# Attention values in two passes, with the row sums of the probabilities taken out of the value product

## The chip, the cores and the metric

The kernel runs on one core of a Trainium2 chip. The metric is the device time of one execution in microseconds (us), lower is better; the median of three runs is given. A core has a matrix engine (TensorE, PE in the profile; PEld is its weight load), a vector engine (VectorE, DVE), an activation engine (ScalarE, ACT), a general engine (GpSimd, POOL) and an engine that issues most transfers (SyncE, SP). Each engine works through its own queue in order; semaphores hold an instruction until those on other engines that it needs are done, and whatever stands behind it on its own queue is held too.

## The reference

A small encoder with two layers on a sequence of 1024 tokens, width 1024, in float32. Layer 0 mixes tokens with a chunked gMLP, layer 1 with chunked attention; each is followed by a gated convolutional feed-forward network. The change touches only the attention of layer 1, with 16 heads of 64 dimensions, where each chunk of 64 queries attends to its own chunk and the 8 chunks before it:

```python
sc = jnp.einsum('bqhd,bkhd->bhqk', qb, kb).astype(jnp.float32) + bias
valid = (start - PAD + jnp.arange(BAND)) >= 0
sc = jnp.where(valid[None, None, None, :], sc, NEG_INF)
p = jax.nn.softmax(sc, axis=-1).astype(vb.dtype)
return jnp.einsum('bhqk,bkhd->bqhd', p, vb)
```

For each query, softmax needs the sum of the exponentials over its keys, and the output is the value product divided by that sum.

## The kernel before

TensorE multiplies in a fast format with fewer mantissa bits (fp32r). To keep float32's accuracy, an operand is split into a high part (the value rounded to the format) and a low part (what is left), and a product is made of three passes: high x high, high x low, low x high. The helper `split` (L137) does this with a cast on ACT (L139) and a subtraction, mostly on DVE (L140).

The attention stage goes over the 16 heads in pairs, since two heads of 64 dimensions fill the 128 partitions: `c` is 0 for the even head of a pair and 1 for the odd one, and `rows[c]` gives the 64 partitions that are its own and the 64 that are the other's. Within a head the loop (from L1396 on) goes over 8 blocks of 128 keys. For a block, `Head.score` makes the scores of up to 640 queries on PE (tile `st`, L1256 and L1258), adds the position bias on DVE for the two near blocks (tile `p`, L1262), takes the exponential on ACT (L1263, L1266), and splits the result: `ph` by ACT (L1269), `pl` by POOL (L1270). Two blocks later (`LAG`) `Head.value` multiplies `ph` and `pl` with the values into the output accumulators `po`, one for each half `t` of the 1024 queries. In between, PE gets work that depends on nothing here: the matmuls `qkv` of the next pair's projections (L181, L184, L188), about 12 per block in an even head and 6 in an odd one, and the matmuls `mx` (L1210, L1217) for the next head's row maxima, which DVE reduces (tiles `junk`, `mb` at L1213, `ma` at L1219).

The order of PE's instructions is written out by hand, with a small clock (`tick`) and work that is put off by some microseconds (`put_off`); the order on DVE, ACT and POOL is set by a scheduler from what each instruction depends on. PSUM has eight tiles here: two for `po`, two for the projections and four (`psS`) that scores, maxima and transposes share. PE can write into one of the four only when its reader on DVE or ACT is done.

In the value product a block takes three passes: VH x ph, VL x ph, VH x pl. VH is 128 columns wide and holds the high part of V in the head's own 64 columns and 1.0 in the other 64; VL holds the low part and 0.0. So the other 64 rows of `po` collect the sums of the probabilities at no extra cost. The transposed V comes from PE four blocks at a time (`vtr`, L1182) and is written by `transpose_v` (L1187, L1188) straight into the even head's tiles; for the odd head it goes to narrow tiles first and from there by transfer (`stage_v`). When a half of a head is done, `Pair.done` copies one row of sums (ACT, L1311) and the head's 64 output rows (DVE, L1315) out of `po`, and after the odd head the sums are turned, inverted, broadcast and multiplied in, and the result is split and stored for the output projection. Three times in a pair POOL also multiplies new weights with their gains (tile `raw`, L159).

## Time and profile before

| | |
|---|---|
| median of 3 runs | 2132.54 us (2130.45 to 2134.04) |
| the profiled execution | 2131.62 us, its span 2129.5 us |
| granted TensorE clock | 0.999 of full speed |
| PE busy | 2116.1 us, 99% of the span |
| DVE busy | 1546.9 us, 73% |
| ACT busy | 1066.3 us, 50% |
| POOL busy | 744.6 us, 35% |
| attention stage | from about 975 to 1409 us |

The profile names a group by line, engine, operation, the tile written and the tiles read, with the shape; `x12` is a count. In the timeline each row starts with the start in us and the duration. Matmuls overlap in the pipeline, and their ends are modelled: how much time one takes is read from the distance of the starts. "Idle before" in brackets is how long the engine had waited, and for whom.

### The profile page before, as it was taken

How to read it: one execution, taken by the hardware profiler on the slowest of the kernel's cores; microseconds unless marked ns; L12 is line 12 of the kernel's file. 1: busy time of each engine (PE TensorE's matmuls, PEld its weight loads, DVE VectorE, ACT ScalarE, POOL GpSimd, SP SyncE). 2: the span in 40 equal slices, each digit the busy share in tenths (PEclk: the TensorE clock that was granted, in tenths of full speed). 3: DMA queues.
4: the chain of work that ended last, by engine and by line, in shares of the span. 5: the costliest groups of instructions: out<-in, count | busy, mean ns of one | idle time of the engine just before them, and what ended most of it. 6: DMA issues, size and time to landing. Idle time of an engine off the chain costs nothing.

```text
span 2129.5 us, 28843 instructions
## 1 busy us (share of the span) xinstructions
PE 2116.1 (99%) x9944; PEld 1771.8 (83%) x9944; DVE 1546.9 (73%) x2313; ACT 1066.3 (50%) x1878; POOL 744.6 (35%) x528
## 2 busy tenths in 40 slices
PE   9999999999999999999999999999999999999998
PEld 8888878888888888878888888888888888888887
DVE  4188789888888857676565665665988888885576
ACT  6333555554445544555555555643645544454443
POOL 1075644332334412054444543421323323342020
PEclk9999999999999999999999999999999999999999
DMA  7267733454445966635555455762244545578653
GB/s 252 80 203 253 242 104 99 139 188 140 172 162 194 299 254 219 238 110 139 132 135 127 127 127 135 186 214 108 79 148 135 187 134 174 164 278 303 213 188 129
DMA packets 181450, 367.86 MB, mean 173 GB/s; under 512 B 42908, under 2 KB 43292, under 8 KB 181304
## 3 DMA queue, kind: packets, MB, share of 16 engines
q1 hardware_dynamic: 177128, 358.47, 52.6%
q10 hardware_dynamic: 4176, 7.55, 1.0%
q8 instruction: 78, 1.28, 0.3%
q14 instruction: 68, 0.56, 0.1%
HBM read 233.12 MB, written 103.40 MB: 158 GB/s over the span
## 4 chain that ended last, share of the span: by engine, by line
PE 93%; DVE 4%; ACT 1%; issue 1%; DMA 0%; POOL 0%; SPq 0%; DVEq 0%; POOLq 0%; ACTq 0%
PE up L995 10%; PE gate L995 10%; PE up L375 7%; PE up L377 7%; PE up L380 7%; PE gate L375 5%; PE gate L380 5%; PE gate L377 5%; PE vps L510 4%; PE qkv L184 4%; PE qkv L181 4%; PE qkv L188 4%; PE ups L181 1%; PE po L1290 1%; PE st L1256 1%; PE po L1288 1%
## 5 line engine op out<-in xcount | busy, mean ns | idle before, releaser
L140 DVE TENSOR_TENSOR wlo<-raw,whi 128x512 fp32r<-128x512 f32 (+1 forms) x395 | 346.5, 883 | 179.7 <-ACT whi L139 179.3
L139 ACT CAST whi<-raw 128x512 fp32r<-128x512 f32 (+1 forms) x395 | 245.1, 623 | 281.1 <-PE gate L995 197.4
L375 PE MATMUL up<-yh,whi 128*128 128x512 f32 x688 | 268.1, 390 | 0.7 <-ACT gate L886 0.6
L377 PE MATMUL up<-yh,wlo 128*128 128x512 f32 x688 | 267.8, 389 | 0.0
L847 POOL TENSOR_TENSOR h<-a 128x512 f32<-128x512 f32 x44 | 82.0, 1864 | 403.3 <-DVE a L839 390.7
L1270 POOL TENSOR_TENSOR pl<-p,ph 128x640 fp32r<-128x640 f32 (+4 forms) x128 | 159.7, 1250 | 173.2 <-ACT ph L1269 128.0
L375 PE MATMUL gate<-th,whi 128*128 128x512 f32 x496 | 192.9, 389 | 0.0
L377 PE MATMUL gate<-th,wlo 128*128 128x512 f32 x496 | 192.9, 389 | 0.0
L380 PE MATMUL up<-yl,whi 128*128 128x512 f32 x688 | 184.2, 389 | 0.0
L375 PEld LDWEIGHTS up<-yh,whi 128*128 128x128 f32 x688 | 129.2, 188 | 28.9 <-ACT gate L886 2.0
L380 PEld LDWEIGHTS up<-yl,whi 128*128 128x128 f32 x688 | 129.1, 188 | 27.3 <-POOL yl L140 0.5
L377 PEld LDWEIGHTS up<-yh,wlo 128*128 128x128 f32 x688 | 129.2, 188 | 26.6
L140 DVE TENSOR_TENSOR yl<-raw,yh 128x512 fp32r<-128x512 f32 x172 | 143.1, 835 | 8.5 <-ACT yh L139 8.1
L184 PE MATMUL qkv<-yh,wlo 128*128 128x512 f32 x336 | 134.3, 400 | 0.0
L380 PE MATMUL gate<-tl,whi 128*128 128x512 f32 x496 | 132.8, 389 | 0.2 <-DVE tl L140 0.2
L181 PE MATMUL qkv<-yh,whi 128*128 128x512 f32 x336 | 132.4, 394 | 0.0
L139 ACT CAST whi<-S 128x512 fp32r<-128x512 f32 x160 | 99.2, 620 | 66.2 <-PE up L380 60.3
L140 DVE TENSOR_TENSOR wlo<-S,whi 128x512 fp32r<-128x512 f32 x160 | 130.6, 817 | 0.0
L995 PE MATMUL up<-yl,whi 128*128 128x512 f32 (+1 forms) x312 | 120.6, 387 | 0.0
L995 PE MATMUL gate<-yh,wlo 128*128 128x512 f32 (+1 forms) x312 | 120.4, 386 | 0.0
L995 PE MATMUL up<-yh,whi 128*128 128x512 f32 (+1 forms) x312 | 120.4, 386 | 0.0
L995 PE MATMUL up<-yh,wlo 128*128 128x512 f32 (+1 forms) x312 | 120.3, 386 | 0.0
(307 smaller groups left out, 5263.7 us busy)
## 6 DMA issues: line engine op xcount, KB each, us to landing
raw<-in_f_win SPq DMA_DIRECT2D x88, 512.0 KB
gT<-h SPq DMA_DIRECT2D x88, 256.0 KB
h<-in_f_wdown SPq DMA_DIRECT2D x44, 512.0 KB
dS<-h SPq DMA_DIRECT2D x88, 256.0 KB
raw<-dS SPq DMA_DIRECT2D x40, 512.0 KB
raw<-gT SPq DMA_DIRECT2D x40, 512.0 KB
gB<-a SPq DMA_DIRECT2D x66, 256.0 KB
raw<-in_f_wdown SPq DMA_DIRECT2D x30, 512.0 KB
```

Of the source, the lines that this page charges most:

```text
L139: behind[S] = S.copy(hi, src)
L140: return eng.tensor_tensor(lo, src, f32(hi), op=ALU.subtract)
L181: nc.tensor.matmul(ps, wh[:, k, :], xs[k][0], start=k == 0, stop=False)
L184: nc.tensor.matmul(ps, wl[:, k, :], xs[k][0], start=False, stop=False)
L188: nc.tensor.matmul(ps, wh[:, k, :], xs[k][1], start=False, stop=k == last)
L375: nc.tensor.matmul(ps, wh[:, k, :], xs[k][0], start=first and k == 0, stop=False, skip_group_check=True)
L377: nc.tensor.matmul(ps, wl[:, k, :], xs[k][0], start=False, stop=False, skip_group_check=True)
L380: nc.tensor.matmul(ps, wh[:, k, :], xs[k][1], start=False, stop=k == 3, skip_group_check=True)
L510: nc.tensor.matmul(ps, a, b, start=k == i == 0, stop=k == KD - 1 and i == 2)
L847: G.tensor_tensor(B[n], x, B.get(y) if isinstance(y, str) else y, op=ALU.subtract)
L995: nc.tensor.matmul(ps[:, cs], w[:, ms], x[:, cs], start=q == i == 0 and p in (1, 6, 5, 4), stop=q == NP - 1 and i == 2, skip_group_check=True)
L1270: marks[2] = G.tensor_tensor(pl[:, :n], pf[:, :n], f32(ph[:, :n]), op=ALU.subtract)
```

## The change

The values are held in one tile per head, V0 for the even head and V1 (two buffers, by turns of the pairs) for the odd one: the high part in the head's own 64 columns, the low part in the other 64. So one pass with `ph` gives the product with both parts, in two halves of the partitions, and a second pass with `pl` is all that is left; `Pair.done` adds the two halves (a copy on ACT, an add on DVE). `transpose_v` writes both heads' tiles directly, and the transfers of `stage_v` are gone.

The sums no longer come out of `po`. After each block of scores the exponentials `p` are added into two sum tiles per head, one for each half of the queries: blocks 0, 2, 4, 6 on POOL, blocks 1, 3, 5, 7 on DVE. The first block is copied into the first tile, and the second tile is set to zero. When a half has all its blocks, its sum tile is split (`sumh`, `suml`), and 2 to 3 us of PE's clock after the half's last value product two matmuls with a tile of ones (`den`, in one of the four shared PSUM tiles) add up the 128 partitions. The rest (`finish`) is as before.

```diff
@@ operand @@
-                parts[p, what] = [b1.tile([P, NB, 64], F32R, tag=f"v{n}", name=f"v{n}") for n in ("hi", "lo")]
+                parts[p, what] = V0, V1[p % 2]
@@ transpose_v @@
-            for c, vh, vl in ((0, VH[0][:, ns, 0:64], VL[0][:, ns, 0:64]), (1, hi[:, ns, :], lo[:, ns, :])):
-                src = ptv[:, :, rows[c][0]]
+            for v, (own, oth) in zip(both, rows):
+                src, vh = ptv[:, :, own], v[:, ns, own]
                 S.copy(vh, src)
-                V.tensor_tensor(vl, src, f32(vh), op=ALU.subtract)
-
-        def stage_v(p):
-            for dst, src in zip((VH[1], VL[1]), parts[p, "v"]):
-                nc.sync.dma_start(f32(dst[:, :, 64:P]), f32(src))
+                V.tensor_tensor(v[:, ns, oth], src, f32(vh), op=ALU.subtract)
@@ Head.__init__ @@
+                self.v = parts[hd // 2, "v"][self.c]
+                self.sum = [b2.tile([P, H], F32, tag=f"sum{t}", name="sum", bufs=1) for t in range(2)]
@@ Head.score @@
                 self.p[kb] = (ph, pl)
+                for t, (a, b) in enumerate(self.ranges(kb)):
+                    if a >= b:
+                        continue
+                    d, e = self.sum[t][:, a - t * H:b - t * H], pf[:, a - q0:b - q0]
+                    if kb == t == 0:
+                        G.tensor_copy(d, e)
+                        G.memset(self.sum[1], 0.0)
+                    else:
+                        (V if kb % 2 else G).tensor_tensor(d, d, e, op=ALU.add)
+                    if kb == (NB - 1 if t else 3):
+                        self.parts = [b2.tile([P, H], F32R, tag=n, name=n, bufs=1) for n in ("sumh", "suml")]
+                        split(*self.parts, self.sum[t])
+
+            def ranges(self, kb):
+                q0 = kb * P
+                end = q0 + min(5, NB - kb) * P
+                return (q0, min(end, H)), (max(q0, H), end)
+
+            def total(self, t):
+                ps = psS("den")
+                for i in range(2):
+                    nc.tensor.matmul(ps, ones_r, self.parts[i], start=i == 0, stop=i == 1)
+                    tick()
+                return ps
@@ Head.value @@
-                    nc.tensor.matmul(d, VH[c][:, kb, :], ph[:, r], start=kb == 0, stop=False, skip_group_check=True)
+                    nc.tensor.matmul(d, self.v[:, kb, :], ph[:, r], start=kb == 0, stop=False, skip_group_check=True)
                     tick(d.shape[1])
-                    nc.tensor.matmul(d, VL[c][:, kb, :], ph[:, r], start=False, stop=False, skip_group_check=True)
-                    tick(d.shape[1])
-                    nc.tensor.matmul(d, VH[c][:, kb, :], pl[:, r], start=False, stop=last, skip_group_check=True)
+                    nc.tensor.matmul(d, self.v[:, kb, :], pl[:, r], start=False, stop=last, skip_group_check=True)
                     tick(d.shape[1])
                     if last:
-                        self.done(c, t, self.po[t])
+                        self.done(c, t, self.po[t], lambda t=t: self.total(t))
@@ Pair.done @@
-                    S.copy(self.den[t][row], po[row])
-                    nc.sync.dma_start(dens[p][t][0][c:c + 1], self.den[t][row])
-                else:
-                    S.copy(self.den[t][own], po[oth])
-                V.tensor_copy(self.o[t][own], po[own])
-                if c == 0:
-                    return
+                S.copy(self.o[t][own], po[oth])
+                V.tensor_tensor(self.o[t][own], po[own], self.o[t][own], op=ALU.add)
+
+                def sums():
+                    if p < LAST:
+                        row = slice(oth.start, oth.start + 1)
+                        S.copy(self.den[t][row], total()[row])
+                        nc.sync.dma_start(dens[p][t][0][c:c + 1], self.den[t][row])
+                    else:
+                        S.copy(self.den[t][own], total()[own])
+                    if c:
+                        self.finish(t)
+                put_off((3.0 if t else 2.0) if p < LAST else 0, sums)
```

Three places show how the instructions now stand, all in the odd head of pair 2 (the numbers in names only tell buffers apart). First PE, at the value product of block 0 and what follows it; before:

```order
L1286 MATMUL po_10562<-ph_10486,vh1_8621 128x512
L1288 MATMUL po_10562<-ph_10486,vl1_8623 128x512
L1290 MATMUL po_10562<-pl_10487,vh1_8621 128x512
L1286 MATMUL po_10566<-ph_10486,vh1_8621 128x128
L1288 MATMUL po_10566<-ph_10486,vl1_8623 128x128
L1290 MATMUL po_10566<-pl_10487,vh1_8621 128x128
```

And now:

```order
L1303 MATMUL po_10642<-ph_10562,v1a_8621 128x512
L1305 MATMUL po_10642<-pl_10563,v1a_8621 128x512
L1303 MATMUL po_10645<-ph_10562,v1a_8621 128x128
L1305 MATMUL po_10645<-pl_10563,v1a_8621 128x128
L184 MATMUL qkv_10548<-yh_8198,wlo_10350 128x512
L188 MATMUL qkv_10548<-yl_8107,whi_10347 128x512
L1287 MATMUL den_10650<-sumh_10516,ones_r_75 128x512
L1287 MATMUL den_10650<-suml_10517,ones_r_75 128x512
```

Two of six matmuls are gone, and the sums of the head before (second half) are multiplied with ones two filling matmuls later.

Second POOL, from the start of the head to block 3; before:

```order
L1270 TENSOR_TENSOR pl_10487<-p_10476,ph_10486 128x640
L1270 TENSOR_TENSOR pl_10520<-p_10509,ph_10519 128x640
L159 TENSOR_TENSOR raw_11144<-raw_11144,cc_68 128x1024
L1270 TENSOR_TENSOR pl_10552<-p_10541,ph_10551 128x640
L1100 MEMSET qe1_8616 1x512
L1270 TENSOR_TENSOR pl_10591<-p_10580,ph_10590 128x640
```

And now:

```order
L1272 MEMSET sum_10551 128x512
L1274 TENSOR_TENSOR sum_10551<-sum_10551,p_10552 128x128
L1271 COPY sum_10550<-p_10552 128x512
L1264 TENSOR_TENSOR pl_10563<-p_10552,ph_10562 128x640
L1264 TENSOR_TENSOR pl_10598<-p_10587,ph_10597 128x640
L159 TENSOR_TENSOR raw_11254<-raw_11254,cc_68 128x1024
L1274 TENSOR_TENSOR sum_10551<-sum_10551,p_10619 128x384
L1274 TENSOR_TENSOR sum_10550<-sum_10550,p_10619 128x256
L1264 TENSOR_TENSOR pl_10630<-p_10619,ph_10629 128x640
L1100 MEMSET qe1_8616 1x512
L1264 TENSOR_TENSOR pl_10674<-p_10663,ph_10673 128x640
```

The work on the sums stands in front of the `pl` of the same block, since it needs `p` only.

Third DVE, from the bias of block 3 to the reductions of block 5; before:

```order
L1262 TENSOR_TENSOR p_10580<-st_10581,bias_10088 128x256
L1213 ISA junk_10599,mb_10493<-mx_10597,bias_10490 128x256
...
L1219 TENSOR_REDUCE ma_10492<-mx_10601 128x1
L1213 ISA junk_10615,mb_10493<-mx_10613,bias_10490 128x256
...
L1219 TENSOR_REDUCE ma_10492<-mx_10617 128x1
L1262 TENSOR_TENSOR p_10620<-st_10621,bias_10088 128x256
L1213 ISA junk_10639,mb_10493<-mx_10637,bias_10490 128x256
...
L1219 TENSOR_REDUCE ma_10492<-mx_10641 128x1
```

And now:

```order
L1256 TENSOR_TENSOR p_10663<-st_10664,bias_10152 128x256
L1205 ISA junk_10688,mb_10572<-mx_10686,bias_10569 128x256
...
L1211 TENSOR_REDUCE ma_10571<-mx_10690 128x1
L1274 TENSOR_TENSOR sum_10551<-sum_10551,p_10663 128x512
L1205 ISA junk_10702,mb_10572<-mx_10700,bias_10569 128x256
...
L1274 TENSOR_TENSOR sum_10550<-sum_10550,p_10663 128x128
L1211 TENSOR_REDUCE ma_10571<-mx_10704 128x1
L1256 TENSOR_TENSOR p_10707<-st_10708,bias_10152 128x256
L1205 ISA junk_10727,mb_10572<-mx_10725,bias_10569 128x256
...
L140 TENSOR_TENSOR suml_10679<-sum_10550,sumh_10678 128x512
L1211 TENSOR_REDUCE ma_10571<-mx_10729 128x1
```

Two adds and the subtraction of a split now stand between the instructions that read the shared PSUM tiles (rows that write one column of `mb` are left out here).

More of the change, by code (lines that the diff above doesn't have):

```diff
@@ L1092, in operand @@
             S.copy(vT, ps)
-            put_off(1.2, lambda: transpose_v(vT, t, hi, lo))
+            put_off(1.2, lambda: transpose_v(vT, t, (hi, lo)))
     def stage(hd, cs):
@@ L1161, in trunk @@
             place.append(b1.tile([P, T], F32R, name=f"{n}1"))
-        VH, VL = ([b1.tile([P, NB, P], F32R, name=f"{n}{c}") for c in range(2)] for n in ("vh", "vl"))
+        V0, *V1 = (b1.tile([P, NB, P], F32R, name=f"v{n}") for n in ("0", "1a", "1b"))
         constant_rows(1, lambda: b2.tile([P, H], F32, tag="o", name="e"))
-        for c in range(2):
-            oth = rows[c][1]
-            G.memset(f32(VH[c][:, :, oth]), 1.0)
-            G.memset(f32(VL[c][:, :, oth]), 0.0)
         def heads():
@@ L1177, in heads, with transpose_v @@
                 w = nw
-        def transpose_v(vT, t, hi, lo):
+        def transpose_v(vT, t, both):
             pt = psS("vtr")
@@ L1276, in value @@
                 q0 = kb * P
-                lo_end = q0 + min(5, NB - kb) * P
-                for t, (a, b) in enumerate(((q0, min(lo_end, H)), (max(q0, H), lo_end))):
+                for t, (a, b) in enumerate(self.ranges(kb)):
                     if a >= b:
@@ L1437, in trunk @@
                 stage(hd + 2, halves[0])
-            if i == (LAG if p < LAST else 5) and c == 0:
-                stage_v(p)
             for _ in range(n // 2):
```

6 lines of the change are left out of this document (3 added, 3 removed).

## The prediction

> **What bounds the kernel now.** I read the busy times first, then the stage table over the attention stage (975 to 1409 us, the one stage that the change touches), then the waits of TensorE (PE) in it.
>
> ```profile
> PE 2116.1 (99%) x9944; PEld 1771.8 (83%) x9944; DVE 1546.9 (73%) x2313; ACT 1066.3 (50%) x1878; POOL 744.6 (35%) x528
> ...
> 975.00:1409.00 434.00, 432.15 (x2307) 374.86 (x2307) 261.01 (x664) 253.85 (x535) 207.93 (x174) 1.00 0.54 136
> ...
> PE st L1256 <- DMA qe<-mr: 0.7, 1, 0.7
> PE po L1290 <- POOL pl L1270: 0.6, 1, 0.6
> PE vtr L1182 <- ACT vT L1092: 0.4, 1, 0.4
> ```
>
> PE is the bound, at a granted clock of 1.00, and in 434 us waits 1.7 us. So each PE microsecond removed is worth one, but only while VectorE (DVE, 261 us busy), ScalarE (ACT, 254) and GpSimd (POOL, 208) stay out of its way. Averages hide the tight place: heads come in pairs, an even head with about 12 filling matmuls to a block of keys (34.1 us) and an odd head with 6 (22.6 us), both with the same softmax work.
>
> ```profile
> 1078.87:1112.99 34.12, 34.12 (x177) 29.30 (x176) 21.07 (x49) 18.06 (x38) 15.15 (x13) 1.00 0.66 159
> 1112.99:1135.64 22.65, 22.65 (x128) 20.00 (x126) 12.91 (x39) 14.30 (x31) 12.29 (x11) 1.00 0.38 88
> 1120.80:1131.10 10.30, 10.30 (x61) 9.30 (x61) 7.31 (x25) 5.80 (x13) 5.83 (x6) 1.00 0.33 77
> ```
>
> Behind the length stand the busy times of PE, PEld, DVE, ACT and POOL. The first row is the even head of pair 2, the second its odd head, the third that head's blocks 3 to 5, where DVE already works 7.31 of 10.30 us.
>
> **PE: what goes and what comes.** The third pass goes: 12 matmuls a head (widths 512, 384, 256, 128, three of each), 192 in all. Their spacing is read from starts, since their modelled ends overlap:
>
> ```profile
> 1118.90 0.40 PE L1286 MATMUL po<-ph,vh 128*128 128x512 f32 x1
> ...
> 1119.60 0.22 PE L1286 MATMUL po<-ph,vh 128*128 128x128 f32 x1
> ...
> 1119.88 0.45 PE L184 MATMUL qkv<-yh,wlo 128*128 128x512 f32 x1
> 1120.17 0.62 PE L188 MATMUL qkv<-yl,whi 128*128 128x512 f32 x2
> ...
> 1122.38 0.34 PE L1286 MATMUL po<-ph,vh 128*128 128x384 f32 x1
> ...
> 1122.91 0.28 PE L1286 MATMUL po<-ph,vh 128*128 128x256 f32 x1
> ...
> 1123.27 0.86 PE L188 MATMUL qkv<-yl,whi 128*128 128x512 f32 x3
> ```
>
> Three passes at 512 take 1118.90 to 1119.60, 0.233 us each; at 384 0.53/3 = 0.177; at 256 0.36/3 = 0.120; at 128, from 1119.60 to 1120.17 less one 512, 0.337/3 = 0.112. One pass of a head is 3 x 0.642 = 1.93 us, times 16 **30.8 us gone**. The multiplication with ones adds 2 matmuls of 512 for each of 2 halves of 16 heads: 64 x 0.233 = **14.9 us back**. Net **-15.9 us**.
>
> The Trainium skill (TensorE: Matmul & The Clock Gate, Back-to-back issue gap) gives n/2.4 + 2.5 ns for an isolated matmul, 56 ns at 128 and 216 at 512; by it the net would be 26.1 - 13.8 = -12.3 us. The spacing here at 128 is twice that, nearer to the 107 ns that the page's weight-load formula makes of 128 columns, and the measured spacing is used.
>
> **What costs nothing.**
>
> ```profile
> vh<-vhi SPq DMA_DIRECT2D x8, 256.0 KB
> vl<-vlo SPq DMA_DIRECT2D x8, 256.0 KB
> L1311 ACT COPY den<-po 1x512 f32<-1x512 f32 x28 | 16.0, 573 | 0.4
> L139 ACT CAST whi<-raw 128x512 fp32r<-128x512 f32 x42 | 25.8, 617 | 13.6 <-PE qkv L188 13.6
> ```
>
> The 16 transfers of V's odd half (SP queue) and four memsets go; no wait of PE above names them. The transposed V is still written by two copies and two subtractions. DVE's copy of a finished half becomes an add of the same 64x512 from PSUM, and ACT gets a copy of some 0.58 us ahead of it, twice a head; ACT has also two casts of 0.62 us a head, 2.4 us in all on 14.30 of 22.65. These are hidden under PE as long as they keep time, which is the next part.
>
> **POOL and DVE: the sums.** Per head POOL gets a memset, a copy of 512 columns and adds of 128, 384, 256, 512, 256; DVE gets adds of 384, 256, 128, 512, 384, 128 and two subtractions of 512. Prices, by the same shapes:
>
> ```profile
> L1270 POOL TENSOR_TENSOR pl<-p,ph 128x640 fp32r<-128x640 f32 x64 | 100.3, 1571 | 73.0 <-ACT ph L1269 61.1 <-PE st L1258 9.0 <-PE po L1290 1.4
> L1270 POOL TENSOR_TENSOR pl<-p,ph 128x384 fp32r<-128x384 f32 x16 | 17.5, 1096 | 24.9 <-ACT ph L1269 22.9 <-PE wo L188 2.0
> L1270 POOL TENSOR_TENSOR pl<-p,ph 128x256 fp32r<-128x256 f32 x16 | 11.8, 737 | 21.1 <-issue 14.2 <-POOL pl L1270 3.1 <-ACT ph L1269 2.4
> L1270 POOL TENSOR_TENSOR pl<-p,ph 128x128 fp32r<-128x128 f32 x16 | 9.3, 578 | 13.0 <-ACT ph L1269 12.2 <-PE st L1256 0.8
> 1045.62 0.68 DVE L1347 TENSOR_TENSOR o<-o,den 128x512 f32<-128x512 f32 x1
> ```
>
> The POOL copy has no row; it lies between a memset (0.52) and a two-input add (1.3), and I take 0.8. What decides is that DVE and POOL do not run such work side by side:
>
> ```profile
> 1033.84 3.10 POOL L1270 TENSOR_TENSOR pl<-p,ph 128x640 fp32r<-128x640 f32 x2
> 1035.97 1.52 DVE L1347 TENSOR_TENSOR o<-o,den 128x512 f32<-128x512 f32 x1
> 1037.00 0.52 POOL L1100 MEMSET qe<- 1x512 f32 x1
> ...
> 1274.37 1.90 POOL L159 TENSOR_TENSOR raw<-raw,cc 128x1024 f32<-128x1024 f32 x1 [1.96 <-DMA raw<-in_w_kv]
> 1274.45 2.36 DVE L140 TENSOR_TENSOR ol<-o,oh 128x512 fp32r<-128x512 f32 x1
> 1276.23 1.47 POOL L1270 TENSOR_TENSOR pl<-p,ph 128x384 fp32r<-128x384 f32 x1
> ```
>
> An instruction of DVE with both inputs in SBUF takes 0.68 us alone. Beside POOL it ends 0.55 us after POOL's instruction does (1037.49 against 1036.94; 1276.81 against 1276.27), and the POOL instruction behind is late in its turn (1.47 us, where its shape takes 1.10 in the mean). Instructions with an input in PSUM (junk, p) keep their time. Every sum on DVE, and both subtractions, are of the kind that waits.
>
> The Trainium skill (SBUF — State Buffer, Who interferes with whom) states this as an exclusive lock, held for the whole instruction, against POOL instructions that read SBUF; the memset at 1037.00, running beside the DVE row, agrees, and for the copy no run here shows it.
>
> **An odd head, walked through.** Time 0 is the first score matmul, 1112.99. Rows of this head before:
>
> ```profile
> 1114.89 0.73 ACT L1269 CAST ph<-p 128x640 fp32r<-128x640 f32 x1
> ...
> 1115.69 1.57 POOL L1270 TENSOR_TENSOR pl<-p,ph 128x640 fp32r<-128x640 f32 x1 [4.20 <-ACT ph L1269]
> 1119.79 1.90 POOL L159 TENSOR_TENSOR raw<-raw,cc 128x1024 f32<-128x1024 f32 x1
> 1123.64 1.56 POOL L1270 TENSOR_TENSOR pl<-p,ph 128x640 fp32r<-128x640 f32 x1
> ```
>
> In the new order POOL's adds stand ahead of the pl of their block. The exponentials of block 0 are there at 1.9 (1114.89 - 1112.99, where ACT's ph began). From there each instruction ends, by the rows above, at: add 2.5, copy 3.3, pl 4.9, two DVE adds (0.7) 5.6, pl 7.2, raw (the next weights' gains) 9.1, adds of 384 and 256 10.8, a DVE add of 512 11.4, pl 13.0, memset 13.5, pl 15.1. Before, POOL was idle 4.2 us in front of the first pl; now it has hardly a gap from 1.9 to 15, and DVE meets it at each sum. In blocks 3 to 5 PE loses (0.177 + 0.120) x 2 + 0.112 + 0.233 = 0.94 of its 10.3 us, leaving 9.36; DVE's 7.31 grow by an add of 512, one of 128, the subtraction and an add of 384 (0.60 + 0.20 + 0.60 + 0.45, from 0.68 at 512 less the overlap of neighbours) to 9.16, before any waiting. The add of 128 asks at 11.9 and waits behind pl until 13.0; the subtraction asks at 14.25 and waits behind the next pl until 15.1. That makes some 11 in 9.4. Behind the two stand on DVE the reductions that free PSUM tiles (only four serve scores, maxima, transposes and now the sums). PE's own times follow from its new order and the spacings above (0.233 for each filling matmul of 512), with its stops added as they come. It stops 0.35 us at the transposes (13.4, tile free at 13.7), 0.9 at the scores of block 5 (15.2, free at 16.1), 0.5 at the second scores of block 3, whose tile is now that of the sums and is read by ACT behind ph, and 0.15 at the first value into the second half, whose predecessor's add stands on DVE behind the first two sums. **1.9 us for an odd head**, against the 1.00 (1.93 - 4 x 0.233) that the head saves. Bounds: 0, if PSUM's slack takes it all, and 3.5, if the 2 us of lock waits come whole on top of the tile waits.
>
> **The other heads.** An even head has slack that the trace shows:
>
> ```profile
> 1096.78 0.40 PE L1258 MATMUL st<-qs,ks 128*128 128x512 f32 x1
> 1098.78 0.41 DVE L1262 TENSOR_TENSOR p<-st,bias 128x256 f32<-128x256 f32 x1
> 1387.88 2.24 DVE L140 TENSOR_TENSOR yl<-raw,yh 128x512 fp32r<-128x512 f32 x2
> 1390.59 2.25 DVE L140 TENSOR_TENSOR yl<-raw,yh 128x512 fp32r<-128x512 f32 x2
> 1384.00:1397.00 13.00, 13.00 (x73) 11.46 (x71) 11.20 (x14) 11.94 (x24) 7.81 (x5) 1.00 0.85 269
> ```
>
> DVE's add came 1.6 us after its matmul's modelled end and PE did not wait. With three more instructions between (0.20 + 0.60 + 0.60) and their lock waits it comes 3 to 4 us late, in periods of 34.12/8 = 4.3: I take 1.0 us a head, bounds 0 and 2.5. Pair 0 has some 5.4 matmuls a block in both heads: 1.5 each. Pair 6's odd head has 3 in its first blocks but no raw: 1.5. In the last pair DVE and ACT are nearly full already (11.20 and 11.94 of 13.00): 2.5 for both heads.
>
> **The sum.** Odd heads of pairs 1 to 5: 5 x 1.9 = 9.5. Even heads of pairs 1 to 6: 6 x 1.0 = 6.0. Pair 0: 3.0. Pair 6's odd head: 1.5. Last pair: 2.5. Together 22.5 us of new PE waits. The profiled execution took 2131.62 us (span 2129.5 and 2.1 around it), 0.9 under the median of 2132.54: 2131.6 - 15.9 + 22.5 = **2138 us**, waits at nothing 2116, all at their upper bounds about 2160.
>
> **Rivals.** *The cover holds.* PSUM's slack and the two-block distance between scores and values take the waits; 0 to 6 us come back: 2116 to 2122, **2118**. For it: 1.7 us of PE waits in the whole stage, and the late add above that cost nothing. Against: 9.16 of 9.36 us in the odd head before any lock. It decides if POOL is through with the pl of block 2 when DVE asks for the sum of block 3, so that nobody queues. *Only the narrow heads pay.* Even heads hide all, odd ones half or more: about 15 us come back, **2131**, no change. *The new waits run away*, as rival on the other end: the adds on POOL in front of pl make the values themselves late by more than the two blocks, each head pays 3 us, 2131.6 - 15.9 + 16 x 3 = **2164**. Against it: my walk has pl of block 4 ready some 2 us before PE asks.
>
> **How the numbers follow.** Forecast 2138 (own range 2130 to 2150), chance 0.50, of it 0.41 above and 0.09 within 0.2%, which is about what a measurement of this kernel can tell (2128.3 to 2136.8). Cover holds: 0.32, faster. Narrow heads only: 0.15, of it 0.11 unchanged and 0.04 faster. Running away: 0.03. So faster 0.36, same 0.20, slower 0.44. Eight times in ten: 2117 to 2150.
>
> **What would show it.** PE's busy time falls by about 16 us whatever else holds. In the odd heads POOL should be gapless from block 0 to 3, the sums on DVE should take 1 to 2 us where they meet pl, and PE should wait for DVE's ma, junk or p and ACT's den in blocks 3 to 6, some 2 us a head. If the waits of PE in the stage stay under 5 us, the forecast is wrong and PSUM's slack was more than I allowed; if PE waits for pl above all, the place is wrong.

## The result, and the profile after

The changed kernel takes **2160.9 us** (median; 2156.4 to 2166.7) against 2131.8 us for the kernel before, run beside it (2130.5 to 2134.0): a ratio of 1.0137, 95% interval 1.0111 to 1.0163. It is 29 us slower; 7 were forecast, and a range up to 2150. The profiled execution took 2156.4 us, its span is 2154.6, 25.1 more than the span of before.

The page's busy times of the changed kernel, and its stretches by pairs and heads (length, then busy time and instructions of PE, PEld, DVE, ACT and POOL, PE's granted clock, the DMA engines' share and GB/s):

```profile
PE 2117.7 (98%) x9816; PEld 1761.3 (82%) x9816; DVE 1622.7 (75%) x2441; ACT 1102.0 (51%) x1942; POOL 837.8 (39%) x636
...
980.04:1026.78 46.74, 42.72 (x220) 34.97 (x218) 37.62 (x88) 30.67 (x66) 35.84 (x35) 1.00 0.32 80
1084.10:1117.35 33.25, 33.25 (x168) 28.37 (x169) 23.03 (x58) 20.48 (x43) 21.06 (x21) 1.00 0.50 138
1117.35:1141.11 23.76, 22.82 (x120) 18.83 (x118) 18.62 (x46) 16.37 (x35) 18.55 (x18) 1.00 0.38 99
1232.38:1260.10 27.72, 24.36 (x119) 20.11 (x118) 21.09 (x46) 16.41 (x35) 17.91 (x18) 0.94 0.33 86
1370.85:1397.45 26.60, 22.29 (x107) 18.16 (x108) 22.46 (x51) 16.89 (x37) 15.97 (x15) 0.94 0.36 91
1397.45:1432.62 35.17, 26.10 (x123) 21.87 (x121) 26.47 (x38) 18.91 (x39) 17.17 (x16) 0.90 0.40 127
1432.62:2154.60 721.98, 715.51 (x3254) 595.28 (x3252) 552.99 (x695) 338.10 (x539) 187.31 (x120) 1.00 0.51 176
```

The rows are pair 0, the even and the odd head of pair 2, the odd head of pair 4, the two heads of the last pair (the second up to its last value product), and all that comes after. The last row took 722.2 us before, so the loss lies in the attention stage and, by 1.2 us, ahead of its first scores. PE's busy time does not tell it: it is 1.6 us higher with 128 matmuls fewer, because a matmul's modelled end moves out when the next one is late or the clock is low. Lengths tell it. Pair 2's even head is 0.9 us shorter than before (34.14, where the saving is 1.00), its odd head 1.1 us longer (22.65).

For every head I took the distance from its first score matmul to that of the next, in both profiled executions, and added the 1.00 us that a head's passes and ones should save:

| stretch | before | after | new waits | forecast |
|---|---|---|---|---|
| start of the stage | 978.8 | 980.0 | 1.2 | 0 |
| pair 0 | 43.2 | 46.7 | 5.5 | 3.0 |
| odd heads of pairs 1 to 5 | 113.2 | 121.7 | 13.5 | 9.5 |
| even heads of pairs 1 to 6 | 205.1 | 201.3 | 2.2 | 6.0 |
| odd head of pair 6 | 20.1 | 21.1 | 2.0 | 1.5 |
| last pair | 46.8 | 61.8 | **17.0** | **2.5** |
| together | | | 41.4 | 22.5 |

41.4 less 15.9 is 25.5, against 25.1 between the spans. The 1.2 us of the first row are no sure part of the change: in the runs below the stage starts between 978.3 and 982.5 us. The last pair alone makes 14.5 of the 18.9 us that were missed.

**An odd head.** PE's timeline in the odd head of pair 2 of the changed kernel (in brackets the idle time before the row, which the modelled ends shorten):

```profile
1125.24 0.28 PE L1252 MATMUL st<-qs,ks 128*128 128x256 f32 x1
1125.57 0.44 PE L1250 MATMUL st<-qe,km 128*128 128x384 f32 x1
...
1129.98 0.28 PE L1303 MATMUL po<-ph,v1a 128*128 128x256 f32 x1
1130.46 0.39 PE L1305 MATMUL po<-pl,v1a 128*128 128x256 f32 x1 [0.20 <-POOL pl L1264]
1130.68 0.34 PE L1303 MATMUL po<-ph,v1a 128*128 128x384 f32 x1
1131.17 0.63 PE L1178 MATMUL vtr<-ident,vT 128*128 128x128 f32 x4 [0.15 <-DVE ma L1211]
...
1132.62 0.34 PE L1209 MATMUL mx<-km,qe 128*128 128x384 f32 x1
1133.45 0.44 PE L1250 MATMUL st<-qe,km 128*128 128x384 f32 x1 [0.49 <-DVE ma L1211]
```

Read from the starts, with 0.12 us for a matmul of 256 columns and 0.18 for one of 384: 0.21 lost at the second scores of block 3, 0.36 at `pl`, 0.31 at the transposes, 0.65 at the scores of block 5.

**A turn that was missed.** Pair 4's odd head is 4 us longer still. The timeline has the same instructions in both heads; first DVE and POOL in pair 2, then DVE, POOL and PE in pair 4:

```profile
1130.83 1.54 POOL L1264 TENSOR_TENSOR pl<-p,ph 128x640 fp32r<-128x640 f32 x1
1131.61 1.31 DVE L140 TENSOR_TENSOR suml<-sum,sumh 128x512 fp32r<-128x512 f32 x1
1132.34 1.72 POOL L1274 TENSOR_TENSOR sum<-sum,p 128x512 f32<-128x512 f32 x1
...
1245.87 1.55 POOL L1264 TENSOR_TENSOR pl<-p,ph 128x640 fp32r<-128x640 f32 x1
1246.65 3.77 DVE L140 TENSOR_TENSOR suml<-sum,sumh 128x512 fp32r<-128x512 f32 x1
1247.38 1.26 POOL L1274 TENSOR_TENSOR sum<-sum,p 128x512 f32<-128x512 f32 x1
1248.62 1.25 POOL L1264 TENSOR_TENSOR pl<-p,ph 128x512 fp32r<-128x512 f32 x1
1250.94 0.44 PE L1250 MATMUL st<-qe,km 128*128 128x384 f32 x1 [2.96 <-DVE ma L1211]
```

In pair 2 `suml` ends 0.55 us after `pl` (1132.92), and POOL's add waits for it (1.72). In pair 4 POOL's add goes first, with its 1.26 us, and so does the `pl` behind it; `suml` ends 0.55 us after that (1250.42). PE stops 2.96 us for the reduction behind `suml`, and then the clock halves, as single microseconds show:

```profile
1252.00:1253.00 1.00, 1.00 (x6) 0.90 (x4) 0.91 (x4) 0.61 (x2) 0.00 (x0) 0.50 0.00 0
...
1254.00:1255.00 1.00, 1.00 (x4) 0.71 (x4) 0.97 (x3) 0.51 (x1) 0.34 (x1) 0.50 0.00 0
```

**The last pair.** The timeline around PE's longest stop:

```profile
1403.07 1.71 DVE L1368 TENSOR_TENSOR o<-o,den 128x512 f32<-128x512 f32 x1
1403.14 0.40 PE L1305 MATMUL po<-pl,v1b 128*128 128x512 f32 x1
...
1404.70 2.07 DVE L140 TENSOR_TENSOR yl<-raw,yh 128x512 fp32r<-128x512 f32 x2
...
1406.70 2.02 DVE L140 TENSOR_TENSOR ol<-o,oh 128x512 fp32r<-128x512 f32 x1
...
1408.76 0.58 ACT L1323 COPY o<-po 64x512 f32<-64x512 f32 x1 [1.18 <-DVE ol L140]
1408.98 2.08 DVE L140 TENSOR_TENSOR yl<-raw,yh 128x512 fp32r<-128x512 f32 x2
...
1410.98 0.67 DVE L1324 TENSOR_TENSOR o<-po,o 64x512 f32<-64x512 f32 x1
...
1411.80 0.45 PE L1303 MATMUL po<-ph,v1b 128*128 128x128 f32 x1 [8.26 <-DVE o L1324]
```

PE wants to start the last head's second accumulator. Its PSUM tile still holds the result of the head before, which ACT and then DVE must take out. ACT's copy writes a buffer `o` that pair 6 still owns: its second half is scaled only at 1403.07 (`o` times `den`) and split at 1406.70 (`ol`). So the copy waits for `ol`, and the add stands behind two more subtractions for output weights (`yl`): 8.26 us, with the clock at 0.50 behind them.

The dependence is not new. The same place in the kernel before, DVE and then PE (`ol` of pair 6, DVE's copy out of the accumulator, the matmul that writes into it next):

```profile
1385.31 1.64 DVE L140 TENSOR_TENSOR ol<-o,oh 128x512 fp32r<-128x512 f32 x1
...
1387.29 0.67 DVE L1315 COPY o<-po 64x512 f32<-64x512 f32 x1
...
1388.19 0.22 PE L1286 MATMUL po<-ph,vh 128*128 128x128 f32 x1
```

There the copy was through at 1387.96, 0.2 us before PE wrote into the tile.

### The profile page after: what moved, and what is told of

It is laid out like the page before. It is cut to its first block, busy times and chain, and to the rows that moved or that the text cites. A ratio compares the mean times of both kernels' runs of the same rounds, so it can differ in the third digit from the quotient of the medians.

```text
span 2154.6 us, 28904 instructions
## 1 busy us (share of the span) xinstructions
PE 2117.7 (98%) x9816; PEld 1761.3 (82%) x9816; DVE 1622.7 (75%) x2441; ACT 1102.0 (51%) x1942; POOL 837.8 (39%) x636
## 3 DMA queue, kind: packets, MB, share of 16 engines
q8 instruction: 77, 1.26, 0.3%
## 4 chain that ended last, share of the span: by engine, by line
PE 87%; DVE 7%; issue 2%; DMA 2%; ACT 1%; POOL 1%; SPq 0%; DVEq 0%; POOLq 0%; ACTq 0%
PE up L995 9%; PE gate L995 9%; PE up L377 7%; PE up L375 7%; PE up L380 7%; PE gate L380 5%; PE gate L375 5%; PE gate L377 5%; PE vps L510 4%; PE qkv L188 3%; PE qkv L184 3%; PE qkv L181 3%; PE ups L181 1%; PE ups L184 1%; PE wo L188 1%
## 5 line engine op out<-in xcount | busy, mean ns | idle before, releaser
L1264 POOL TENSOR_TENSOR pl<-p,ph 128x640 fp32r<-128x640 f32 (+4 forms) x128 | 164.2, 1283 | 62.4 <-ACT ph L1263 39.1
```

The costliest lines, as they stand in the source:

```text
L1264: marks[2] = G.tensor_tensor(pl[:, :n], pf[:, :n], f32(ph[:, :n]), op=ALU.subtract)
```

## The experiments

All times are medians, with the ratio to the kernel before and its interval; lengths come from the profiled execution of each run, by the same starts of score matmuls. 2116 us is what the forecast's sum gives without any new wait.

**1. The sums of pair 6 at once.**

```diff
-                put_off((3.0 if t else 2.0) if p < LAST else 0, sums)
+                put_off((3.0 if t else 2.0) if p < LAST - 1 else 0, sums)
```

> As the changed kernel, but the sums of pair 6 are multiplied with ones at once instead of 2 and 3 us of the program's clock later. Late-chain theory: that delay pushed the scaling and splitting of pair 6's second half two blocks back, so its buffer o was still in use when the even head of the last pair wanted to empty its second accumulator, and TensorE stopped 8.3 us and then ran at half the granted clock. It expects the stop under 2 us, no drop of the clock in the last pair, and 2161 - 11 = about 2150 us. Rival, VectorE too full in the last pair whatever the order: the stop stays above 5 us and the time at 2157 to 2163.

2152.8 us, 1.0093 (1.0073 to 1.0112). DVE and PE in the last head of this run:

```profile
1400.10 0.68 DVE L1368 TENSOR_TENSOR o<-o,den 128x512 f32<-128x512 f32 x1
...
1402.57 0.95 DVE L140 TENSOR_TENSOR ol<-o,oh 128x512 fp32r<-128x512 f32 x1
...
1406.33 0.67 DVE L1324 TENSOR_TENSOR o<-po,o 64x512 f32<-64x512 f32 x1
...
1407.14 0.44 PE L1303 MATMUL po<-ph,v1b 128*128 128x128 f32 x1 [3.79 <-DVE o L1324]
```

The stop falls from 8.26 to 3.79 us, the last pair from 61.8 to 56.5, the time by 8 us. The chain is a cause, though not the whole stop. The same profile has the 3.77 us `suml` in two odd heads (pairs 1 and 2), each with 2.96 us of stop: 28.3 and 27.5 us long, the others 22.9 to 23.5. One missed turn costs some 4.5 us with the clock behind it; the profile of the changed kernel has one of them, this one two, by the same instructions in the same order.

**2. The sums left out, everything else in place.**

```diff
-                        G.tensor_copy(d, e)
-                        G.memset(self.sum[1], 0.0)
-                    else:
-                        (V if kb % 2 else G).tensor_tensor(d, d, e, op=ALU.add)
+                        G.memset(self.sum[0], 1.0)
+                        G.memset(self.sum[1], 1.0)
```

> As the changed kernel, but all adds of the sums and the first copy are left out (both sum tiles are set to ones instead, so the denominators are wrong); the multiplication with ones, the splits and the copies on ScalarE stay. If the sums and the waits of VectorE and GpSimd for each other make the losses of the odd heads: the stops in the odd heads of pairs 1 to 5 fall from 2 us to under 0.5 us each, these heads take 21.7 us, and what is left above 2116 us is the stop of the last pair: 2120 to 2130 us. Rival, the new order around the accumulators (copy on ScalarE, then add on VectorE) makes the losses: odd heads still above 23 us and 2145 us or more.

2134.7 us, 1.0016 (1.0006 to 1.0025), between the two expectations. The adds are worth 26 us; but some 19 us above 2116 are left without them. Even heads take 33.1 us, as the 1.00 us saved predicts, odd ones still 22.9, pair 0 43.2 and the last pair 54.4. What is left: in each odd head 0.34 us for a score tile that DVE has not read yet, and 0.7 us at the end of an odd head, where the next head's first scores wait for the DMA of the row maxima (`qe<-mr`), now that PE comes there earlier; and a stop of 6.29 us at the last head's accumulator.

**3. All adds on VectorE.**

```diff
-                        (V if kb % 2 else G).tensor_tensor(d, d, e, op=ALU.add)
+                        V.tensor_tensor(d, d, e, op=ALU.add)
```

> As the changed kernel, but every add of the sums is on VectorE (GpSimd keeps the first copy and the memset). VectorE gets five more adds a head, some 2.0 us of own time, GpSimd loses 4.3 us a head. Lock theory (VectorE loses more by waiting for GpSimd than by its own work): GpSimd has gaps again, VectorE's instructions with two inputs in SBUF come down from 1.2 to 2 us to 0.7 to 1.0, odd heads 23 us or less, 2145 to 2155 us. Load theory (VectorE simply has too much work): odd heads 25 us, 2168 us or more.

2156.7 us, 1.0121 (1.0106 to 1.0136). Groups of `suml` on DVE between 1022 and 1306 us, first of the changed kernel, then of this one:

```profile
L140 DVE TENSOR_TENSOR suml<-sum,sumh 128x512 fp32r<-128x512 f32 x19 | 19.2, 1009 | 3.6 <-ACT sumh L139 3.4
```

```profile
L140 DVE TENSOR_TENSOR suml<-sum,sumh 128x512 fp32r<-128x512 f32 x20 | 16.3, 815 | 3.6 <-ACT sumh L139 3.4
```

The odd heads of pairs 1 to 5 take 117.2 us together for 121.7, and `suml` gets shorter. But the missed turn of pair 4 makes nearly all of this: without its 3.77 us `suml` took 0.86 us in the mean in the changed kernel, and the other four odd heads take 94.0 us there and 93.9 here. Of DVE's other adds those of 128 columns got shorter (0.63 to 0.42 us in the mean), those of 384 longer (0.55 to 0.74). So five more adds a head on DVE cost nothing in these heads, where the load theory said 25 us a head; the lock theory's 23 us was missed too (23.4), and so was its range for the time. Pair 0 grows from 46.7 to 50.4, and the odd head of pair 6 from 21.1 to 23.4: there load is the likelier cause, but no run separates the two.

**4. The adds behind the low part instead of ahead of it.**

```diff
-                        (V if kb % 2 else G).tensor_tensor(d, d, e, op=ALU.add)
+                        with tc.issue_after(marks[2].ins):
+                            (V if kb % 2 else G).tensor_tensor(d, d, e, op=ALU.add)
```

> As the changed kernel, but each add of the sums is issued behind the low part (pl) of its block instead of ahead of it. If the adds ahead of pl make the values late: the waits of TensorE for pl in the odd heads (0.4 to 0.7 us each) go, about 3 us in five heads, 2156 to 2158 us. If it is VectorE's turn that matters and not GpSimd's order: VectorE's adds meet the next pl instead, the waits for ma stay or grow, 2160 to 2166 us.

2160.3 us, 1.0133 (1.0118 to 1.0148): no change. The waits for `pl` go; PE waits for `mx<-mb` instead, 1.35 to 2.02 us in four of five odd heads. POOL's order was not the limit.

**5. The low part of the finished sums on GpSimd** (on top of 1).

```diff
-                        split(*self.parts, self.sum[t])
+                        split(*self.parts, self.sum[t], G)
```

> On top of the run with pair 6's sums at once: the low part of each finished sum (suml) is subtracted on GpSimd instead of VectorE. In the run before it two odd heads had a stop of 2.96 us with the clock at half speed behind it, each 4.5 us, where suml on VectorE waited 3.8 us through three GpSimd instructions on end. If that missed turn makes these stops: none of them is left, the runs lie within 4 us of each other, about 2145 us, the fastest run of the kernel without this edit. Rival, any VectorE instruction with two inputs in SBUF can miss its turn: stops of 2 us and more in odd heads again, at other instructions, 2148 to 2155 us.

2157.5 us, 1.0127 (1.0112 to 1.0142). The stops of 2.96 us at `suml` are gone, but an add misses its turn and makes one of 3.21; POOL, DVE and PE in the odd head of pair 0:

```profile
1018.40 1.56 POOL L1264 TENSOR_TENSOR pl<-p,ph 128x640 fp32r<-128x640 f32 x1
1018.54 4.41 DVE L1274 TENSOR_TENSOR sum<-sum,p 128x512 f32<-128x512 f32 x1
1019.93 1.25 POOL L140 TENSOR_TENSOR suml<-sum,sumh 128x512 fp32r<-128x512 f32 x1
1021.15 1.25 POOL L1264 TENSOR_TENSOR pl<-p,ph 128x512 fp32r<-128x512 f32 x1
...
1023.35 0.39 PE L1202 MATMUL mx<-km,qe 128*128 128x256 f32 x1 [3.21 <-DVE mb L1205]
```

The add was issued beside the first `pl` and came behind two more instructions of POOL, 0.55 us after the end of the last (1022.95 against 1022.40). The rival is right: it is not `suml` alone, an add with two inputs in SBUF can miss its turn beside a POOL without gaps as well. The other odd heads up to pair 6 have stops of up to 1.64 us.

**6. Adds by pair:** VectorE in pairs 1 to 6, GpSimd in pairs 0 and 7 (on top of 1).

```diff
-                        (V if kb % 2 else G).tensor_tensor(d, d, e, op=ALU.add)
+                        (V if 0 < self.hd // 2 < LAST else G).tensor_tensor(d, d, e, op=ALU.add)
```

> On top of the run with pair 6's sums at once: all adds on VectorE in pairs 1 to 6 (where that made odd heads 23.2 us without long stops) and all on GpSimd in pairs 0 and 7 (where VectorE is full). Lock theory: odd heads 23.2, pair 0 and the last pair shorter than with sums by turns (46.7 and 62 us) by 2 to 5 us together, 2141 to 2145 us. Rival: GpSimd's adds make the values late in pair 0 and 7 (waits of TensorE for pl of 1 us and more), 2148 us or more.

2150.4 us, 1.0093 (1.0078 to 1.0108). Odd heads 120.0, pair 0 46.9, the last pair 58.6 (56.5 in run 1): with the adds on POOL, PE waits for `suml` (up to 1.95 us) and `pl`. No gain that can be told from run 1.

**7. Even heads alone in two passes.** The odd heads have three passes and ones in the tile, as before; for room `p` has two buffers and `vT` one. In a second run both have their buffers back (the split sums share those in which V is staged) and the last pair's adds are on GpSimd; in a third all other adds are on VectorE, the row maxima are transposed earlier, and pair 6 is scaled earlier (see 8 and 9).

```diff
+                    v = (VH if c else V0)[:, kb, :]
+                    nc.tensor.matmul(d, v, ph[:, r], start=kb == 0, stop=False, skip_group_check=True)
                     tick(d.shape[1])
...
+                    if c:
+                        nc.tensor.matmul(d, VL[:, kb, :], ph[:, r], start=False, stop=False, skip_group_check=True)
+                        tick(d.shape[1])
+                    nc.tensor.matmul(d, v, pl[:, r], start=False, stop=last, skip_group_check=True)
...
-                    if a >= b:
+                    if a >= b or c:
                         continue
```

> Two passes and sums for the even heads alone; the odd heads keep three passes, with ones in the stationary tile and V staged by the SP queue as in the kernel before. For room in SBUF the tile p has two buffers instead of three and vT one instead of two. If the even heads hide all the new work and only odd heads and the chain behind them pay (in the run without sums an even head took 33.1 us for 34.1 before, an odd one 22.9 for 22.6): even heads 33.2 us, odd heads 22.6 as before (the two multiplications with ones that fall into them add 0.5, so 23.1), the stop of the last pair under 1 us, 2131.6 - 4 to 7 = 2125 to 2128 us. Rival, the sums cost wherever they stand (locks and fuller queues): no gain, 2131 to 2138 us.

> Again two passes for the even heads alone, but with three buffers of p and two of vT as in the other kernels: the split sums share the buffers in which V of the odd head is staged (in the last pair, those of the operands' halves). The adds of the last pair are all on GpSimd and its multiplications put off by 2 and 3 us. If the two buffers of p made the even heads' stops of 1.0 to 1.5 us for mb in the run before: even heads 33.3 us instead of 34.9, odd 22.9, 2153 - 6 x 1.5 - about 5 in pair 0 and the last pair = 2136 to 2141 us, and below 2131 only if pair 0 and the last pair come back to their times of before. Rival, staging V by DMA and sums together slow the even heads: stops for mb stay at 1 us, 2148 to 2153 us.

> Two passes in the even heads alone (three buffers of p), adds of pairs 0 to 6 all on VectorE, row maxima early, pair 6 scaled early. If the stop of 1.0 us in each even head came from two adds on VectorE that waited out GpSimd's pl (2.14 us for the two, 0.89 in the changed kernel): even heads 33.3 us, odd 22.9, last pair 3 to 5 us shorter, 2144 - 7 - 4 = 2133 us, 2130 to 2136. Rival, VectorE misses its turn at other adds: even heads 34.4 us or more, 2139 us or more.

2153.0 us, 1.0107 (1.0090 to 1.0124); with three buffers of `p` 2144.4, 1.0055 (1.0042 to 1.0069); with the third set of edits 2152.6, 1.0102 (1.0085 to 1.0119). My expectation failed each time. Odd heads take 22.9 us in all three, as they should; it is the even heads that grow, to 35.1, 34.6 and 35.9 us in the mean. DVE, POOL and PE in the even head of pair 1, second run:

```profile
1039.26 2.02 POOL L1272 TENSOR_TENSOR pl<-p,ph 128x640 fp32r<-128x640 f32 x1
1039.89 2.14 DVE L1282 TENSOR_TENSOR sum<-sum,p 128x128 f32<-128x128 f32 x2
...
1045.67 0.44 PE L1217 MATMUL mx<-km,qe 128*128 128x384 f32 x1 [1.05 <-DVE mb L1213]
```

The two adds (of 128 and 512 columns) took 0.89 us in the changed kernel, because they met no `pl` there. A stop of 1.0 us for `mb` stands at the same place in pairs 1 to 5. So the even heads of the changed kernel do not seem safe by their slack alone: where the order on DVE and POOL shifts by a microsecond or two, the gain is gone. That the meeting with `pl` makes this stop is argued from these rows; the staging of V, which comes back with these runs, is not excluded. The third run was badly made: with the early transposition PE waits 1.4 to 2.1 us for the row maxima (`mr <- DVE mb`) in five of the six even heads, so it says nothing on the adds. What it does show is a last head of 25.3 us, as before (25.1), where that head has no sums and pair 6 is scaled early.

**8. Without sums, with the chains mended.** First pair 6 at once and the row maxima's transposition put off by 2.0 us from block 5 (before: 0.5 us from block 6); then also the third output weight loaded two blocks later, and the next three one block later; then, in place of that, pair 6 scaled earlier.

```diff
-                if i == (6 if p < LAST - 1 else 5):
-                    put_off(0.5 if p < LAST - 1 else 2.0, mx.row)
+                if i == 5:
+                    put_off(2.0, mx.row)
...
-        loads = [0, 2, 8, 10, 11, 12]
+        loads = [0, 2, 10, 11, 12, 13]
...
-                waits = (8.0, 8.0) if stays else (9.0, 9.0 if p < LAST - 1 else 6.5)
+                waits = (8.0, 8.0) if stays else (9.0, 9.0 if p < LAST - 1 else 2.5)
```

> As the run with the sums left out (denominators wrong), with pair 6's multiplications at once and the transposition of a head's row maxima (mr) put off by 2 us from block 5 instead of 0.5 us from block 6, in all pairs. Without sums 2134.65 us were left, 18 above the 2116 of TensorE's work. If 8 of these are the chain in the last pair (6.29 us stop and the clock) and 4 the wait for the DMA of the row maxima at the head of the next head (0.56 us in each odd head of pairs 1 to 6, 0.8 in pair 0 and 1): 2122 to 2125 us, odd heads 22.2 us. Rival, the time sits in what both kernels have in common (accumulator emptied by two engines): above 2130 us.

> As the run without sums, with pair 6's multiplications at once and early row maxima (denominators wrong, 2127.8 us), and the load of the third output weight, with its two casts on ScalarE and two subtractions on VectorE, moved from block 0 of the last head to block 2 (loads 2, 10, 11, 12, 13). If these casts and subtractions, standing ahead of the emptying of the accumulator, make the 4.0 us stop that is left: stop under 1 us, clock 1.0 in the last head, 2121 to 2123 us. Rival, the scaling of pair 6 (o times den, ol) alone holds the buffer o: stop stays above 3 us, 2127 us.

> As the run without sums, with pair 6's multiplications at once and early row maxima (denominators wrong, 2127.8 us), and pair 6's second half scaled 2.5 us of the program's clock behind its reciprocals instead of 6.5, so that ol is split before the even head of the last pair is through. If the buffer o held by pair 6 makes the 4.0 us stop: the stop is under 1 us, no drop of the clock in the last head, from its first score to its last value product 25 to 26 us instead of 29.8, 2122 to 2124 us. Rival, the copy on ScalarE and the add on VectorE queue behind other work anyway: stop above 2.5 us, 2127 us.

2127.8 us, 0.9981 (0.9972 to 0.9991); 2128.3, 0.9982 (0.9973 to 0.9991); 2126.3, 0.9978 (0.9969 to 0.9987). The row maxima explain most of the odd heads' loss (22.1 us instead of 22.9, where 21.65 was the aim), and pair 0 takes 40.6 instead of 43.2. The weights do not explain the stop at the accumulator, the buffer does. DVE and PE with the weights later, and DVE with pair 6 scaled early:

```profile
1377.33 1.85 DVE L1366 TENSOR_TENSOR o<-o,den 128x512 f32<-128x512 f32 x1
...
1383.75 0.67 DVE L1322 TENSOR_TENSOR o<-po,o 64x512 f32<-64x512 f32 x1
...
1384.57 0.30 PE L1301 MATMUL po<-ph,v1b 128*128 128x128 f32 x1 [3.98 <-DVE o L1322]
```

```profile
1372.19 0.69 DVE L1366 TENSOR_TENSOR o<-o,den 128x512 f32<-128x512 f32 x1 [2.46 <-DMA den<-rden]
...
1378.10 0.68 DVE L1322 TENSOR_TENSOR o<-po,o 64x512 f32<-64x512 f32 x1 [1.83 <-ACT o L1321]
```

In the second the stop is gone (no wait of PE for `o` above 0.4 us) and the clock stays at 1.00 in the last head. The last pair takes 51.7 us, 54.9 in the first of these runs. The median moves by 1.5 us only, which these runs cannot tell from nothing: other waits (for `pl` 1.24, for `ph` 0.70) come up in the last head.

**9. The full computation with these mends:** adds by pair, pair 6 at once, row maxima early; in one run the output weights later, in the other pair 6 scaled early. In both the last pair's even head is multiplied with ones 2 and 3 us later.

```diff
-                put_off((3.0 if t else 2.0) if p < LAST else 0, sums)
+                put_off((3.0 if t else 2.0) if p < LAST - 1 or p == LAST and c == 0 else 0, sums)
```

> The full computation with all that helped so far: pair 6's multiplications at once, row maxima early, output weights later, adds on VectorE in pairs 1 to 6 and on GpSimd in pairs 0 and 7, the last pair's even head multiplied 2 and 3 us later (no stop for suml). From 2150.4 us of the run by pair: row maxima -4, last pair -8 (the stops of 2.0, 1.6, 2.5 and 1.4 us there and the clock behind them): 2138 us, 2135 to 2142. Rival, VectorE stays full in the last pair and its work only moves: 2146 us or more. Faster than the kernel before (2131) only if the odd heads lose less than 1 us each to the sums.

> The full computation with pair 6's multiplications at once, early row maxima, adds by pair as before and pair 6 scaled early (the output weights stay where they were). If the buffer o is the cause: the stop of the last head falls under 1.5 us, 2147 - 5 = 2142 us. If VectorE's and GpSimd's load in the last pair is: the last pair takes 57 us as before, 2146 to 2148 us.

2147.1 us, 1.0072 (1.0058 to 1.0086), and 2147.8, 1.0074 (1.0059 to 1.0089). These two and the better of the runs of 7 lie closest to the kernel before among those that compute everything, and are still slower. With pair 6 scaled early the stop for `o` is gone here too (with the weights later it is 0.40 us), and the last pair stays at 56.6 us: PE waits for the transposes' tile (1.90), the row maxima (1.52), `pl` (1.48) and `suml` (1.13) instead. Against the same mends without sums (2126.3) the sums cost 21.5 us. No version that computes everything beat the kernel before.

## Why the prediction was wrong

**The sign and most of the places were right, a term was not.** The failed step is "In the last pair DVE and ACT are nearly full already (11.20 and 11.94 of 13.00): 2.5 for both heads": it measured 17.0. I costed the last pair by its load and did not follow the deferred sums to who comes after. They are put off by up to 3 us, behind them stand two trips through DMA, the scaling and the split, all at fixed distances; so pair 6 gives its buffer `o` back two blocks later, and that buffer is what ACT's new copy needs before the accumulator is free, as DVE's copy did before, with 0.2 us to spare. The cost of ACT's copy was put at nothing, "as long as they keep time"; here it did not.

Run 1 shows that 5.3 of the 17 us hang on this delay, and the runs without sums show that the buffer is the link. The profiles of the other runs agree. Counted from the first score of the last head, the scaling (`o` times `den`) starts at 0.9 us in the kernel before and at 5.6 us in the changed one. In the runs with two passes in all heads a start at -1.1 and -0.1 us goes with no stop at the accumulator, 0.8 with 0.4 us, 2.8 to 2.9 with 2.5 to 4.0, and 5.3 to 6.8 with 6.3 to 8.5. (The first two runs of experiment 7, with another order in the odd heads, stop 2.0 and 2.3 us at 0.9 and 1.5.) A third buffer for `o`, the direct test, was not run.

Of the rest, 6.9 us are there without sums too, with that stop gone (51.7 us, where 46.8 less 2.0 was the aim). With the sums back and the stop gone it is 56.6 us, so 4.9 come with their load; these parts are from different runs and need not add up. In the 51.7 us PE has seven waits of 0.36 to 1.24 us, 4.9 us together (for a score tile, the transposes, an output weight, the row maxima, `ph` and twice `pl`), where the kernel before has two of 1.1 us together. Why they come up there is not settled.

**Odd heads: place and mechanism right.** The walk named four stops: the transposes (0.35), the scores of block 5 (0.9), the second scores of block 3 (0.5), the first value into the second half (0.15). Pair 2 shows 0.31, 0.65, 0.21 and none, and 0.36 at `pl`, which the walk had ready in time. DVE's sums beside POOL were forecast at 1 to 2 us and took 1.2 to 1.3; POOL is gapless from 1124.85 to 1135.3, that is in blocks 3 to 5; in blocks 0 to 3, where the forecast had it gapless, it stood idle 0.56 and 0.86 us, and it ends 18.55 of 23.76 us busy. The copy on POOL, taken at 0.8, took 0.63 in the mean. The sum of the five heads is 13.5 for 9.5: some 4 of it is the one missed turn with its clock, which nothing in the profile of before showed.

**Even heads: 2.2 us for 6.0.** Here the two rivals in which even heads hide their waits were right in the changed kernel; most of the 2.2 stands in pair 4 (34.7 us, the others 33.3 to 33.5). Experiment 7 suggests on how little it rests.

**Pair 0: 5.5 for 3.0,** and 1.2 ahead of it. Without sums pair 0 takes 43.2 us, so 3.5 come with them, and with early row maxima 40.6, so 2.7 hang on the maxima's latency. That is 0.7 more than the 5.5, since its two heads then save 2.7 us and not 2.0.

**The net of -15.9 on PE holds where nothing else waits:** without sums an even head takes 33.1 us for 34.14. That PE's busy time would fall by 16 us was wrong; modelled ends fill short waits, so busy time is no measure of saved matmuls.

**The rival that "runs away"** had the nearest time (2164), by another mechanism: PE waits 1.7 us for `pl` in the whole run, and moving the adds behind `pl` gained nothing. The "about 2160" of all upper bounds is as near, by luck: the bounds given (3.5 and 2.5 us a head) add to 32.5 us and 2148, the other 12 us have no bound in the text, and the measured waits lie elsewhere (even heads 2.2 of 15, last pair 17.0). The forecast would have been wrong in its place if PE waited for `pl` above all; it did not.

## What to carry to other kernels

When work is put off, follow the tile at its far end: the cost is paid by the next owner of that buffer, which may be the accumulator that TensorE needs empty, and not by the engine that was late. Look in the profile of before for how much that owner has to spare; here it was 0.2 us. In the odd heads the saving on TensorE was lost where VectorE and GpSimd instructions that read SBUF met; count those that are queued behind each other, not the busy shares. First run the change with its side work left out: here that gave none of the 16 us at once (2134.7 us), and 5 with the chains mended (2126.3).

## What the runs showed of the hardware

A VectorE instruction with two inputs in SBUF can be passed over. In pair 4 `suml` was issued while GpSimd's first `pl` ran, and two more GpSimd instructions went ahead of it (3.77 us for 0.68); the add of experiment 5 took 4.41 us in the same way. The Trainium skill (SBUF — State Buffer, Who interferes with whom) gives the shared ports to whoever issues first, for the whole instruction, and lets the other wait; pair 2's 1.31 us agrees, the 3.77 us of pair 4 and of run 1 (twice) do not.

TensorE's clock can halve after stops that are quite short, and need not. Before the next row, a stretch in the even head of the last pair, PE had stopped 2.06 us for the transposes' tile:

```profile
1380.00:1385.00 5.00, 4.77 (x20) 4.26 (x21) 4.39 (x11) 3.12 (x7) 3.49 (x3) 0.66 0.52 158
```

0.66 over 5 us is 3.4 us at half clock, some 1.7 us of work lost for a 2 us stop; after the 2.96 us stop it was 0.50 for 3.4 us as well. In the first run of experiment 8, stops of 0.69 and 0.36 us, one behind the other in the even head of the last pair, were followed by 3.4 us at 0.50; in its other two runs the same two stops (0.70 and 0.36, 0.69 and 0.36) left the clock at 1.00. So did a stop of 2.02 us in experiment 4 (pair 3) and three of 2.04 to 2.10 in the third run of experiment 7, where a fourth of 2.09 did not. The length of the stop alone does not decide here; what does, these runs do not show. The Trainium skill (TensorE: Matmul & The Clock Gate, What's actually happening) gives one idle window of about 3.4 us as the condition; the length at half clock agrees with that window, the condition does not, since none of these stops is that long. In the kernel before the clock was 1.00 over this stage.
